# Two more pairs of w_down by seven products: pair 7 also in the first runs of the first two thirds

## The chip, the cores and the metric

The kernel runs on one core of a Trainium2 chip. The metric is the device time of one execution in microseconds, the median of several runs. Five engines matter: TensorE (PE, and PEld for its weight loads), VectorE (DVE), ScalarE (ACT), GpSimd (POOL) and SyncE (SP), whose queue issues nearly all of the DMA transfers.

## The reference

One decoder layer on 256 tokens of width 2048, in float32. An RMS norm feeds one input projection; from its columns come eight attention heads and a pooling mixer; both go through w_out into the residual stream x. Then the part that the change is about:

```python
def conv_ffn(h, w_up, conv_w, conv_b, w_down):
    u = h @ w_up
    ...
    for i in range(CONV_WIDTH):
        y = y + conv_w[i] * u_pad[:, i:i + S]
    gate, val = jnp.split(y, 2, axis=-1)
    return (jax.nn.silu(gate) * val) @ w_down
```

w_up is 2048 x 11264 and w_down 5632 x 2048. The layer's result is x + conv_ffn(rms_norm(x)).

## The kernel before

**Products in three parts.** Every float32 operand is split into a high part, rounded to the format fp32r that TensorE reads fast, and a low part, the rest. A product is then three matmuls: high x high, high x low, low x high. The high part of a weight chunk is written by ScalarE (`high`, L181), the low part by VectorE (`low`, L186), which also releases the chunk's raw tile, so that the next load can start.

**Chunks and steps.** The weights arrive in chunks of 128 x 2048 numbers (1 MB), in an order that `plan` (L71) writes out. There are four raw tiles, and a fifth once the first part of the program has closed. Split chunks lie in four tiles (high) and three tiles (low). The main loop (L1046) goes through steps u, two to a chunk. At a step that begins a chunk it writes, in this order: what is due in `firsts`; `high` of the chunk three ahead and `low` of the chunk two ahead; a `make`, if one is placed there; what is due in `agenda`, where `later(n, f)` puts f for n steps on; what is `deferred`; and then the step's own matmuls. Each engine works in the order written.

**The feed-forward part** goes through the 22 groups of 256 hidden columns in three thirds of 8, 8 and 6 groups (THIRDS). A third first computes its groups (`gate` and `value`, L822 and L836): up-projection, convolution of width 3 over the tokens, SiLU, product, split into high and low parts in the tile hid, where group j is pair j of row blocks of w_down. Then come two runs over the pairs, nb = 0 and nb = 1, one for each half of the 2048 output columns.

**Eight or seven products.** A pair of row blocks and 1024 output columns make a 2 x 2 block product. A dense pair (`eight_products`) issues eight products of 128 x 128 by 128 x 512, 24 matmuls. A pair of the other kind (`seven_mixed` and `seven_rest`) forms seven products in the manner of Strassen and Winograd, 21 matmuls. For that it needs two things:

- Sums of the left factors, four of them, 128 x 128 each (`left_sums`, L874): four operations of VectorE on the tile y of the group, a copy to the high part on ScalarE, and the low part on VectorE.
- Sums of the right factors. `make` (L194) loads a 1 MB block of mix, adds quarters in three operations of VectorE, and stores the result in mixed[i]. It is done ahead, at chunks named in EARLY (before the first third) and PLACES (within the thirds). Later a pair loads it as its "sum" chunk, and then a "rest" chunk of 128 x 1536, one step each. A dense pair loads one chunk of two steps.

SEVEN names the pairs with seven products in each run: pairs 1 to 6 in the first and 1 to 7 in the second run of the first two thirds, 0 to 4 and 0 to 3 in the last third, 35 in all. `down_order` (L66) gives the order: the first run goes through the pairs from 0 up, so that a dense pair 0 comes first and a dense pair 7 last; the second run takes the pairs with seven products first.

**The last group of a third** (pair 7) is finished while the first run is under way. In the last third, where the flag at_once holds, its steps are: the convolution in two halves at steps 2 and 4 of the run, the taps at 6, the product with the gate at 7, the low part of hid at 8. In the first two thirds it goes another way (convolution at once, taps at step 4, product at 6, low part at 8), and the sums of pair 7 follow 16 steps after that, in the second run. The line for it, in `rest2` (L868):

```python
                f = lambda: late.__setitem__(("S", j), left_sums(y, end, at_once))
                later(16, f) if end else f()
```

The sums of all pairs live in six tiles with the tag "sums"; those of pair 7 take the tile that pair 1 has left.

Of the kernel before, what the change touches and what calls it, by code (L numbers as in the profile page):

```python
# [23 lines left out]
F32 = mybir.dt.float32  # L24
# [29 lines left out]
THIRDS = ((0, 8), (8, 16), (16, 22))  # L54
SEVEN = 2 * (((1, 2, 3, 4, 5, 6), (1, 2, 3, 4, 5, 6, 7)),) + (((0, 1, 2, 3, 4), (0, 1, 2, 3)),)
EARLY = (37, 38, 40, 42, 44)
PLACES = ((2, 2.5, 3, 3.5, 4, 4.5, 5, 6, 6.5), (0, 0.5, 1, 1.5, 2, 2.5, 3, 4, 4.5, 5, 6, 6.5), (0, 0.5, 1, 1.5, 2, 2.5, 3, 3.5, 4))
# [7 lines left out]

def down_order(size, sevens, nb):  # L66

    return [*sevens, *(j for j in range(size) if j not in sevens)] if nb else list(range(size))


def plan():  # L71

    rows = [(k, i) for i, k in enumerate(24 * ["tok"] + 25 * ["feat"])]
    makes, t = list(EARLY), 0
    for (g0, g1), sevens, places in zip(THIRDS, SEVEN, PLACES):
        c = rows[-1][1] + 1
        makes += [len(rows) + 4 * int(p) + (5 if p % 1 else 2) for p in places]
        rows += [("feat", c + i) for i in range(4 * (g1 - g0))]
        c = rows[-1][1] + 1
        for nb in range(2):  # L80
            for i, j in enumerate(down_order(g1 - g0, sevens[nb], nb)):
                seven = j in sevens[nb]
                if seven:
                    rows.append(("sum", t))
                    t += 1
                rows.append(("rest" if seven else "tok", c + nb * (g1 - g0) + i))
    assert len(makes) == t, (len(makes), t)
    return rows, makes
# [12 lines left out]
def layer(ctx: ExitStack, tc: tile.TileContext, xT, wts, mix, par, rel_d, ident_d, icnt_d, out):  # L101
# [590 lines left out]
    def open_late():  # L692
        ectx.close()
        pool = ctx.enter_context(tc.tile_pool(name="late", bufs=1))
        late["pool"] = pool
        late["prow"] = pool.tile([P, 8], F32, name="prow", tag="prow")
        late["qrow"] = pool.tile([32, 3, 8], F32, name="qrow", tag="qrow")
        late["x2f"] = [block("x2f").rearrange("p (k t) -> p k t", t=S) for _ in range(4)]
        for k0, k1 in ((0, 2), (2, 4), (4, 8), (8, 12), (12, KT)):
            nc.sync.dma_start(x2_tiles(k0, k1), xT[:, KT + k0 * S:KT + k1 * S].rearrange("p (k t) -> p k t", t=S))  # L700
        late["sq"] = pool.tile([P, 2, S], F32, name="sq2", tag="y1")
        late["u"] = pool.tile([P, 2, 2 + S], F32, name="u")
        nc.gpsimd.memset(late["u"][:, :, :2], 0.0)
        free.append(f"raw{RAWS}")
        load_next()

    def x2_tiles(k0, k1):
# [114 lines left out]
    def gate(ps, g):  # L822
        if g == 0:
            stats2()
        conv_in(ps)

# [9 lines left out]
    def value(ps, g, j, seven, end, at_once):  # L836
# [31 lines left out]
        def rest2(y, hid, ks):  # L868
            nc.vector.tensor_tensor(hid[:, ks, 1, :], y, hid[:, ks, 0, :].bitcast(F32), op=OP.subtract)
            if seven:  # L870
                f = lambda: late.__setitem__(("S", j), left_sums(y, end, at_once))
                later(16, f) if end else f()

    def left_sums(y, alone, at_once):  # L874

        s = y.rearrange("p a (b n) -> p (a b) n", n=P)
        parts = block("sums", F32R).rearrange("p (a b n) -> p a b n", a=2, n=P)
        for out_, a, b, op in ((3, 3, 1, OP.subtract), (1, 0, 1, OP.subtract), (0, 3, 0, OP.add), (2, 2, 0, OP.subtract)):
            nc.vector.tensor_tensor(s[:, out_, :], s[:, a, :], s[:, b, :], op=op)
        pending.append(lambda: nc.scalar.activation(parts[:, 0], s, AF.Copy))  # L880
        low_part = lambda: nc.vector.tensor_tensor(parts[:, 1], s, parts[:, 0].bitcast(F32), op=OP.subtract)
        if alone:
# [4 lines left out]
        else:  # L887
            firsts.setdefault(now[0] + 4, []).append(low_part)
        return parts

# [9 lines left out]
    def seven_mixed(u, j, run, first):  # L900
# [3 lines left out]
        del wparts[c]  # L904
        s2, s3, _, s1 = (tuple(late["S", j][:, a, i, :] for a in range(2)) for i in range(4))
        a22 = tuple(late["hid"][:, 2 * j + 1, a, P:] for a in range(2))
# [6 lines left out]
    def seven_rest(u, j, run, first, last):  # L913
# [4 lines left out]
        a11, a12 = (tuple(late["hid"][:, 2 * j + k, a, :P] for a in range(2)) for k in range(2))  # L918
        s4 = tuple(late["S", j][:, a, 2, :] for a in range(2))
        c0 = run["c"][0]  # L920
# [9 lines left out]
    def seven_sums(run, a):  # L930
# [7 lines left out]
        if run["n"]:  # L938
            b = scratch("sb")
        else:  # L940
            b = late["pool"].tile([P, 2, S], F32, name="sb", tag="y0")
        b = b.rearrange("p a n -> p (a n)")
# [35 lines left out]
    for n, ((g0, g1), sevens) in enumerate(zip(THIRDS, SEVEN)):  # L978
        ups = []
        for g in range(g0, g1):  # L980
            ups.append(feat_block(lambda: late["h"], XK, lambda ps, g=g: gate(ps, g)))
            ups.append(feat_block(lambda: late["h"], XK,
                                  lambda ps, g=g, j=g - g0, sevens=sevens, end=g == g1 - 1: value(ps, g, j, any(j in s for s in sevens), end, sevens[0][0] == 0 and g >= g1 - 2)))
        u0 = len(steps)
# [4 lines left out]
        for nb in range(2):  # L989
# [19 lines left out]
            fresh0 = {(t, b) for t in range(NT) for b in range(2)}  # L1009
            js = down_order(g1 - g0, sevens[nb], nb)  # L1010
            for j in js:
# [68 lines left out]
def chunks(w_in, pool_w, w_out, w_up, w_down):  # L1080
# [27 lines left out]
    for (g0, g1), sevens in zip(THIRDS, SEVEN):  # L1108
        for g in range(g0, g1):
            out += feat(w_up, 256 * g, XK) + feat(w_up, DFF + 256 * g, XK)  # L1110
        for nb in range(2):
            for j in down_order(g1 - g0, sevens[nb], nb):
                out += pair(w_down, 2 * (g0 + j), 1024 * nb, j in sevens[nb])
# [38 lines left out]
```

## Time and profile before

| what | value |
|---|---|
| median of three runs | 984.37 us (984.16 to 985.06) |
| the profiled execution | 984.03 us |
| span of its instructions | 982.2 us |
| PE / DVE / ACT / POOL busy | 977.5 / 873.6 / 628.1 / 60.8 us |
| bytes moved by DMA | 311.31 MB, 317 GB/s on average |
| first, second, last down stage | 78.22, 78.23 and 57.95 us of matmuls, from 458.46, 710.80 and 919.63 us on |

The page gives the busy time of each engine, then 40 slices of the span, the DMA queues, the chain of work that ended last, and the costliest groups of instructions. In a group's line stand the line of the kernel, engine, operation, what it writes and reads, the count, the busy time and the mean length, and the idle time of the engine before it with what ended it. A timeline gives start, length and operation of one engine in order of time; "x2" merges neighbours of one kind, and square brackets show an idle time before the operation.

### The profile page before, as it was taken

The numbers are of one execution on the slowest core, as the hardware profiler recorded it, in microseconds if no ns is written. First come the engines' busy times: TensorE is split into PE (matmuls) and PEld (weight loads), VectorE is DVE, ScalarE is ACT, GpSimd is POOL, SyncE is SP. The second block draws the span as 40 slices with busy tenths as digits, with TensorE's granted clock in tenths as the row PEclk, the third lists the DMA queues.
The fourth block names the chain that finished last, engine by engine and source line by source line (L and its number), as shares of the span: only waits on it lengthen the run. The fifth ranks groups of instructions, "written<-read, shape, count | busy, mean of one in ns | idle before, by whom it ended". The sixth has DMA issues, their size and how long they took to land.

```text
span 982.2 us, 13594 instructions
## 1 busy us (share of the span) xinstructions
PE 977.5 (100%) x5255; PEld 846.4 (86%) x5255; DVE 873.6 (89%) x950; ACT 628.1 (64%) x734; POOL 60.8 (6%) x118
## 2 busy tenths in 40 slices
PE   9999999999999999999999999999999999999998
PEld 7888888898888888888888888888888888888887
DVE  6776859887978999998999999999889999999898
ACT  6655445454556766777766666767686756767762
POOL 0202322200002310000000000000000000000000
PEclk9999999999999999999999999999999999999999
DMA  9959776589968999987999999888779999998684
GB/s 350 317 203 314 244 250 204 204 316 381 333 258 289 303 390 398 361 326 249 353 345 363 343 382 380 355 329 349 268 276 358 371 348 357 386 356 346 211 347 166
DMA packets 51713, 311.31 MB, mean 317 GB/s; under 512 B 7016, under 2 KB 9704, under 8 KB 19904
## 3 DMA queue, kind: packets, MB, share of 16 engines
q1 hardware_dynamic: 46960, 298.51, 80.7%
q0 software_dynamic: 4688, 11.94, 4.1%
q8 instruction: 41, 0.67, 0.3%
q14 instruction: 24, 0.20, 0.1%
HBM read 265.46 MB, written 44.96 MB: 316 GB/s over the span
## 4 chain that ended last, share of the span: by engine, by line
PE 99%; DMA 0%; DVE 0%; SPq 0%; ACT 0%; issue 0%; DVEq 0%
PE ps_feat L271 41%; PE ps_down L894 22%; PE ps_feat L273 21%; PE ps_tok L259 9%; PE ps_val L249 4%; PE ps_pool L280 1%; PE ps_s L492 1%; DMA raw<-in_wts 0%; PE ps_av L528 0%; PE ps_av L530 0%; PE ps_val L240 0%; DVE x L1000 0%; SPq L153 0%; ACT wh L161 0%; PE ps_feat L268 0%; PE ps_row L404 0%
## 5 line engine op out<-in xcount | busy, mean ns | idle before, releaser
L271 PE MATMUL ps_feat<-x2h,wh 128*128 128x512 f32 x1406 | 478.2, 389 | 0.0
L190 DVE TENSOR_TENSOR wl<-raw,wh 128x2048 fp32r<-128x2048 f32 (+1 forms) x180 | 390.4, 2181 | 12.9 <-ACT wh L184 5.2
L184 ACT ACTIVATE wh<-raw 128x2048 fp32r<-128x2048 f32 (+1 forms) x180 | 329.3, 1834 | 99.6 <-DMA raw<-in_wts 52.8
L273 PE MATMUL ps_feat<-x2h,wl 128*128 128x256 f32 x1408 | 389.1, 276 | 0.0
L271 PEld LDWEIGHTS ps_feat<-x2h,wh 128*128 128x128 f32 x1406 | 264.0, 188 | 54.7
L273 PEld LDWEIGHTS ps_feat<-x2h,wl 128*128 128x128 f32 x1408 | 264.3, 188 | 0.0
L894 PE MATMUL ps_down<-wh,hid 128*128 128x512 f32 (+1 forms) x358 | 122.0, 387 | 0.0
L162 DVE TENSOR_TENSOR wl<-raw,wh 128x2048 fp32r<-128x2048 f32 (+3 forms) x44 | 83.0, 1895 | 37.8 <-ACT wh L161 28.9
L894 PE MATMUL ps_down<-wh,sums 128*128 128x512 f32 x280 | 98.6, 389 | 0.0
L540 ACT ACTIVATE fs<-ps_feat 128x512 f32<-128x512 f32 x52 | 31.1, 597 | 105.5 <-PE ps_feat L273 54.4
L271 PE MATMUL ps_feat<-cat,wh 128*128 128x512 f32 x256 | 87.3, 390 | 0.0
L811 ACT ACTIVATE z<-u,pv 128x256 f32<-128x256 f32 x176 | 79.3, 498 | 3.3 <-DVE x L937 3.3
L259 PE MATMUL ps_tok<-wh,xh 128*128 128x512 f32 x256 | 80.1, 392 | 0.0
L894 PEld LDWEIGHTS ps_down<-wh,hid 128*128 128x128 f32 x358 | 67.0, 188 | 13.8
L161 ACT ACTIVATE wh<-raw 128x2048 fp32r<-128x2048 f32 (+3 forms) x44 | 69.3, 1597 | 10.6 <-DMA raw<-in_wts 7.0
L273 PE MATMUL ps_feat<-cat,wl 128*128 128x256 f32 x256 | 70.8, 276 | 0.0
L894 PE MATMUL ps_down<-wl,hid 128*128 128x512 f32 (+1 forms) x179 | 69.3, 387 | 0.0
L819 DVE TENSOR_TENSOR y<-y,z 128x512 f32<-128x512 f32 x88 | 60.6, 688 | 4.4
L894 PEld LDWEIGHTS ps_down<-wh,sums 128*128 128x128 f32 x280 | 52.6, 188 | 10.9
L271 PEld LDWEIGHTS ps_feat<-cat,wh 128*128 128x128 f32 x256 | 48.1, 188 | 9.9
L259 PEld LDWEIGHTS ps_tok<-wh,xh 128*128 128x128 f32 x256 | 48.1, 188 | 9.9
L543 DVE TENSOR_TENSOR fs<-ps_feat,fs 128x512 f32<-128x512 f32 x52 | 35.8, 689 | 22.0 <-ACT fs L540 21.9
(184 smaller groups left out, 1076.2 us busy)
## 6 DMA issues: line engine op xcount, KB each, us to landing
raw<-in_wts SPq DMA_DIRECT2D x143, 1024.0 KB, 7.5
raw<-in_mix SPq DMA_DIRECT2D x35, 1024.0 KB, 7.4
mixed<-raw SPq DMA_DIRECT2D x35, 1024.0 KB, 7.5
raw<-mixed SPq DMA_DIRECT2D x35, 1024.0 KB, 6.2
raw<-in_wts SPq DMA_DIRECT2D x35, 768.0 KB, 6.1
raw<-in_wts SPq DMA_DIRECT2D x4, 512.0 KB, 7.2
x2d<-x2x POOLq DMA_DIRECT2D x4, 512.0 KB, 7.9
x<-x2d POOLq DMA_DIRECT2D x32, 64.0 KB, 6.5
```

Source lines behind the costliest of these rows:

```text
L161: nc.scalar.activation(wh, w, AF.Copy)
L162: nc.vector.tensor_tensor(wl, w, wh.bitcast(F32), op=OP.subtract)
L184: nc.scalar.activation(w, raws[c][:, :width(c)], AF.Copy)
L190: nc.vector.tensor_tensor(wl, raws[c][:, :width(c)], wh.bitcast(F32), op=OP.subtract)
L249: nc.tensor.matmul(ps[b][:, t, :], xh[:, k, a, ts], w[:, ws], start=False, stop=(k == KT - 1 and n == 2), skip_group_check=True)
L259: nc.tensor.matmul(ps[:, t, :], act[:, k0 + k, a, ts], w[:, ws], start=(first and k == 0 and n == 0), stop=(last and k == 1 and n == 2))
L271: nc.tensor.matmul(ps, wh[:, ws], act[:, k, :, :], start=(bool(first) and n == 0), stop=False, skip_group_check=True)
L273: nc.tensor.matmul(ps[:, S:], wl[:, ws], act[:, k, 0, :], start=False, stop=(last and n == len(ks) - 1), skip_group_check=True)
L543: nc.vector.tensor_tensor(dst, ps[:, :, :S], dst, op=OP.add)
L811: nc.scalar.activation(z[i][:, m, :], u[:, m, 1 - i:1 - i + S], AF.Copy, scale=cw[1 - i])
L819: nc.vector.tensor_tensor(y, y, t, op=OP.add)
L894: nc.tensor.matmul(ps, a, w, start=(first and n == 0), stop=(last and n == 2), skip_group_check=True)
```

## The change

Pair 7 becomes a pair with seven products in the first runs of the first two thirds too: 37 sets in all. Both runs of these thirds go through pairs 1 to 7 and then the dense pair 0, so the first run begins with a pair of seven products. Two more makes are needed and are placed at chunks 16 and 27. In the first two thirds the end of a third takes the steps of the last third (at_once holds there too), and the sums of pair 7 follow one step after the low part of hid instead of 16. They lie in two tiles of their own, with the tags "u" (the high part) and "y0" (the low part); so u is made anew in each third, and a scratch tile of the first run takes the tag "y1" instead of "y0".

```diff
-SEVEN = 2 * (((1, 2, 3, 4, 5, 6), (1, 2, 3, 4, 5, 6, 7)),) + (((0, 1, 2, 3, 4), (0, 1, 2, 3)),)
-EARLY = (37, 38, 40, 42, 44)
+SEVEN = 2 * (2 * ((1, 2, 3, 4, 5, 6, 7),),) + (((0, 1, 2, 3, 4), (0, 1, 2, 3)),)
+EARLY = (16, 27, 37, 38, 40, 42, 44)
...
-def down_order(size, sevens, nb):
+def down_order(size, sevens):

-    return [*sevens, *(j for j in range(size) if j not in sevens)] if nb else list(range(size))
+    return [*sevens, *(j for j in range(size) if j not in sevens)]
...
+    def new_u():
+        late["u"] = late["pool"].tile([P, 2, 2 + S], F32, name="u", tag="u")
+        nc.gpsimd.memset(late["u"][:, :, :2], 0.0)
...
     def gate(ps, g):
         if g == 0:
             stats2()
+        elif any(g == g0 for g0, _ in THIRDS):
+            new_u()
...
                 f = lambda: late.__setitem__(("S", j), left_sums(y, end, at_once))
-                later(16, f) if end else f()
+                later(1, f) if end else f()
...
     def left_sums(y, alone, at_once):
...
-        parts = block("sums", F32R).rearrange("p (a b n) -> p a b n", a=2, n=P)
+        if alone:
+            pair = [late["pool"].tile([P, n], F32R, name="sums7", tag=tag)[:, :512] for n, tag in ((516, "u"), (512, "y0"))]
+        else:
+            parts = block("sums", F32R)
+            pair = [parts[:, :512], parts[:, 512:]]
+        pair = [t.rearrange("p (b n) -> p b n", n=P) for t in pair]
...
-            b = late["pool"].tile([P, 2, S], F32, name="sb", tag="y0")
+            b = late["pool"].tile([P, 2, S], F32, name="sb", tag="y1")
...
-                                  lambda ps, g=g, j=g - g0, sevens=sevens, end=g == g1 - 1: value(ps, g, j, any(j in s for s in sevens), end, sevens[0][0] == 0 and g >= g1 - 2)))
+                                  lambda ps, g=g, j=g - g0, sevens=sevens, end=g == g1 - 1: value(ps, g, j, any(j in s for s in sevens), end, g >= g1 - 2)))
```

More of the change, by code (lines that the diff above doesn't have):

```diff
@@ L80, in plan @@
         for nb in range(2):
-            for i, j in enumerate(down_order(g1 - g0, sevens[nb], nb)):
+            for i, j in enumerate(down_order(g1 - g0, sevens[nb])):
                 seven = j in sevens[nb]
@@ L701, in open_late @@
         late["sq"] = pool.tile([P, 2, S], F32, name="sq2", tag="y1")
-        late["u"] = pool.tile([P, 2, 2 + S], F32, name="u")
-        nc.gpsimd.memset(late["u"][:, :, :2], 0.0)
+        new_u()
         free.append(f"raw{RAWS}")
         load_next()
+    def new_u():
+        late["u"] = late["pool"].tile([P, 2, 2 + S], F32, name="u", tag="u")
+        nc.gpsimd.memset(late["u"][:, :, :2], 0.0)
     def x2_tiles(k0, k1):
@@ L824, in gate @@
             stats2()
+        elif any(g == g0 for g0, _ in THIRDS):
+            new_u()
         conv_in(ps)
@@ L871, in rest2 @@
                 f = lambda: late.__setitem__(("S", j), left_sums(y, end, at_once))
-                later(16, f) if end else f()
+                later(1, f) if end else f()
     def left_sums(y, alone, at_once):
         s = y.rearrange("p a (b n) -> p (a b) n", n=P)
-        parts = block("sums", F32R).rearrange("p (a b n) -> p a b n", a=2, n=P)
+        if alone:
[4 more added lines that the diff above has]
+        pair = [t.rearrange("p (b n) -> p b n", n=P) for t in pair]
         for out_, a, b, op in ((3, 3, 1, OP.subtract), (1, 0, 1, OP.subtract), (0, 3, 0, OP.add), (2, 2, 0, OP.subtract)):
             nc.vector.tensor_tensor(s[:, out_, :], s[:, a, :], s[:, b, :], op=op)
-        pending.append(lambda: nc.scalar.activation(parts[:, 0], s, AF.Copy))
-        low_part = lambda: nc.vector.tensor_tensor(parts[:, 1], s, parts[:, 0].bitcast(F32), op=OP.subtract)
+        pending.append(lambda: nc.scalar.activation(pair[0], s, AF.Copy))
+        low_part = lambda: nc.vector.tensor_tensor(pair[1], s, pair[0].bitcast(F32), op=OP.subtract)
         if alone:
@@ L888, in left_sums @@
             firsts.setdefault(now[0] + 4, []).append(low_part)
-        return parts
+        return pair
     def product(ps, left, right, first, last):
@@ L904, in seven_mixed @@
         del wparts[c]
-        s2, s3, _, s1 = (tuple(late["S", j][:, a, i, :] for a in range(2)) for i in range(4))
+        s2, s3, _, s1 = (tuple(t[:, i, :] for t in late["S", j]) for i in range(4))
         a22 = tuple(late["hid"][:, 2 * j + 1, a, P:] for a in range(2))
@@ L918, in seven_rest @@
         a11, a12 = (tuple(late["hid"][:, 2 * j + k, a, :P] for a in range(2)) for k in range(2))
-        s4 = tuple(late["S", j][:, a, 2, :] for a in range(2))
+        s4 = tuple(t[:, 2, :] for t in late["S", j])
         c0 = run["c"][0]
@@ L1009, in layer @@
             fresh0 = {(t, b) for t in range(NT) for b in range(2)}
-            js = down_order(g1 - g0, sevens[nb], nb)
+            js = down_order(g1 - g0, sevens[nb])
             for j in js:
@@ L1111, in chunks @@
         for nb in range(2):
-            for j in down_order(g1 - g0, sevens[nb], nb):
+            for j in down_order(g1 - g0, sevens[nb]):
                 out += pair(w_down, 2 * (g0 + j), 1024 * nb, j in sevens[nb])
```

## The prediction, before the changed kernel ran

> **What bounds the kernel now.** I read the page first, for the busy time of each engine and the chain that ended last.
>
> ```profile
> span 982.2 us, 13594 instructions
> ...
> PE 977.5 (100%) x5255; PEld 846.4 (86%) x5255; DVE 873.6 (89%) x950; ACT 628.1 (64%) x734; POOL 60.8 (6%) x118
> ...
> PE 99%; DMA 0%; DVE 0%; SPq 0%; ACT 0%; issue 0%; DVEq 0%
> ```
>
> TensorE runs from end to end and is 99% of the chain. The list of waits, for TensorE alone, has two lines, both from the start of the program:
>
> ```profile
> PE ps_start L323 <- DVE ones L311: 1.1, 1, 1.1
> PE ps_val L240 <- ACT wh L161: 0.3, 1, 0.3
> ```
>
> So time falls only if TensorE gets fewer matmuls, and rises only if something makes TensorE wait. VectorE, at 89%, is the engine with the least to spare. The chain in order of time gives the three down stages (start, us):
>
> ```profile
> 458.46 78.22 PE ps_down L894 x345
> 710.80 78.23 PE ps_down L894 x345
> 919.63 57.95 PE ps_down L894 x255
> ```
>
> 78.22 / 345 = 0.227 us from one matmul to the next. This is the price I use; the mean of 389 ns that the groups give for such a matmul is its length, and lengths overlap.
>
> **What is removed.** A dense pair issues 24 matmuls of 512 columns, a seven-product pair 21. Pair 7 changes from 24 to 21 in the first run of the first two thirds: 2 x 3 x 0.227 = 1.36 us less on TensorE, all of it on the path. In the Trainium skill, TensorE: Matmul & The Clock Gate, section Back-to-back issue gap, gives about 131 ns as the sustained spacing at 512 columns. By that the saving would be 0.79 us; the rows of this trace have 0.227, and they decide.
>
> **What moves: the sums of pair 7.** These are the left factors of its products, made by VectorE (four small operations, a ScalarE copy to the high part, one operation for the low part). Before, they were made 16 steps later, in the second run, and used there:
>
> ```profile
> 519.43 1.26 DVE L879 TENSOR_TENSOR y<-y 128x128 f32<-128x128 f32 x4
> ...
> 525.41 0.69 DVE L881 TENSOR_TENSOR sums<-y,sums 128x512 fp32r<-128x512 f32 x1
> ```
>
> Now the first run needs them. I count its steps from 0: pairs 1 to 7 take two steps each (0 to 13), pair 0 follows at 14 and 15. Pair 7's up-projection ends just before step 0; by the code its chain goes: convolution from step 2, taps at 6, the product with the gate at 7, low part of hid at 8, the four sums at 9, their low part at 11. At each step VectorE first splits the weight chunk two steps ahead. TensorE wants the low part of the sums as weights of the third matmul of step 12. VectorE works in the order written, so that low part stands behind the splits of chunks 12 and 13. The question is when VectorE gets there.
>
> The first run of the last third is the model: it starts with a seven-product pair already, and its end group runs the same steps up to the low part of hid, without the sums. Its VectorE timeline (start, us, operation, idle before):
>
> ```profile
> 913.67 1.27 DVE L879 TENSOR_TENSOR y<-y 128x128 f32<-128x128 f32 x4
> 914.86 1.75 DVE L190 TENSOR_TENSOR wl<-raw,wh 128x1536 fp32r<-128x1536 f32 x1
> ...
> 920.30 0.69 DVE L543 TENSOR_TENSOR fs<-ps_feat,fs 128x512 f32<-128x512 f32 x1 [2.29 <-ACT fs L540]
> ...
> 921.63 3.95 DVE L190 TENSOR_TENSOR wl<-raw,wh 128x2048 fp32r<-128x2048 f32 x2
> 925.50 0.69 DVE L881 TENSOR_TENSOR sums<-y,sums 128x512 fp32r<-128x512 f32 x1
> 926.10 7.83 DVE L190 TENSOR_TENSOR wl<-raw,wh 128x2048 fp32r<-128x2048 f32 x4
> 934.63 2.29 DVE L190 TENSOR_TENSOR wl<-raw,wh 128x2048 fp32r<-128x2048 f32 x1 [0.70 <-ACT wh L184]
> 936.84 1.41 DVE L819 TENSOR_TENSOR y<-y,z 128x512 f32<-128x512 f32 x2
> 938.17 1.75 DVE L190 TENSOR_TENSOR wl<-raw,wh 128x1536 fp32r<-128x1536 f32 x1
> 939.84 0.68 DVE L843 TENSOR_TENSOR y<-y 128x512 f32<-128x512 f32 x1
> 940.45 2.28 DVE L190 TENSOR_TENSOR wl<-raw,wh 128x2048 fp32r<-128x2048 f32 x1
> 942.65 0.68 DVE L869 TENSOR_TENSOR hid<-y,hid 128x512 fp32r<-128x512 f32 x1
> 943.25 2.28 DVE L190 TENSOR_TENSOR wl<-raw,wh 128x2048 fp32r<-128x2048 f32 x1
> ```
>
> And TensorE there: the run's first matmul, the first one five pairs later, and one place in the second run:
>
> ```profile
> 919.46 0.40 PE L894 MATMUL ps_down<-wh,sums 128*128 128x512 f32 x1
> ...
> 943.29 0.39 PE L894 MATMUL ps_down<-wh,hid 128*128 128x512 f32 x1
> ...
> 953.72 0.48 PE L894 MATMUL ps_down<-wl,sums 128*128 128x512 f32 x1
> 954.03 0.39 PE L894 MATMUL ps_down<-wh,sums 128*128 128x512 f32 x1
> ```
>
> VectorE's side, from start to start in these rows: a split of 2048 takes 2.20 (940.45 to 942.65), of 1536 1.67 (938.17 to 939.84), the four sums 1.19 (913.67 to 914.86). From 943.25 on, the changed kernel does the split of chunk 11 (now 1536 wide, 1.67), the sums (1.19), chunk 12 (2.20), chunk 13 (1.67), the low part (0.69): 7.42, so it ends at 950.67 on the model's clock. TensorE's side: five pairs took 943.29 - 919.46 = 23.83, or 4.77 a pair, so step 12 begins at 919.46 + 28.60 and its third matmul at 948.51. How fast TensorE follows VectorE, and what its weight load adds:
>
> ```profile
> 951.36 2.28 DVE L190 TENSOR_TENSOR wl<-raw,wh 128x2048 fp32r<-128x2048 f32 x1
> ...
> L894 PEld LDWEIGHTS ps_down<-wl,sums 128*128 128x128 f32 x140 | 26.3, 188 | 5.6 <-DVE wl L190 0.2
> ```
>
> That split ended at 953.64, its matmul began at 953.72: 0.08. With 0.19 for the load, the third matmul starts at 950.67 + 0.27 = 950.94 instead of 948.51. **A stall of 2.43 us, in each of two thirds: 4.86 us.** Every later matmul is queued behind it.
>
> Bounds. VectorE stood idle for 0.70 ahead of 934.63, waiting for ScalarE's high part; without that the stall is 1.73. If a weight chunk landed that much later again, 3.1. I take the model's own value, since the order of work is the same.
>
> **What else moves, at nothing.** The two runs start with a seven-product pair instead of a dense one. The model starts so, and its chain of 57.95 us runs through that start unbroken; if that cover were thin, the cost is of the size of the gap after 953.72, under 0.1. The new places of the sums (the buffers of u and of the gate's y, both read out by step 7) and the fresh u of each third are tile names with one memset of two columns on GpSimd, 6% busy. The dense pair at a run's end stands where one stood before.
>
> **What is added: two more makes**, at chunks 16 and 27. Each is one load and one store of 1 MB and three operations of VectorE:
>
> ```profile
> L198 DVE TENSOR_TENSOR raw<-raw 128x1024 f32<-128x1024 f32 x35 | 42.6, 1218 | 0.0
> L200 DVE TENSOR_TENSOR raw<-raw 128x512 f32<-128x512 f32 x35 | 24.2, 692 | 1.2
> L199 DVE TENSOR_TENSOR raw<-raw 128x512 f32<-128x512 f32 x35 | 24.2, 692 | 1.2
> ```
>
> 2.60 us each. Where they fall, and one run to come back to (window, PE, PEld, DVE busy; last DMA share and GB/s):
>
> ```profile
> 88.29:97.79 9.50, 9.50 (x46) 8.00 (x45) 2.29 (x1) 3.86 (x3) 0.00 (x0) 1.00 0.87 322
> 153.00:194.00 41.00, 41.00 (x243) 36.39 (x243) 36.92 (x57) 20.50 (x27) 10.41 (x19) 1.00 0.64 218
> 497.76:531.08 33.32, 33.32 (x149) 27.59 (x147) 32.19 (x26) 23.98 (x15) 0.00 (x0) 1.00 0.95 351
> ```
>
> VectorE is idle for 7.2 of the 9.5 us that follow the first place, and for 4.1 of the 41 after the second; DMA has room in both. SP's queue gets the store, which waits for VectorE there with the next loads behind it, and the raw tile is out of the rotation until it has landed. I cost both at nothing; uncovered it is 2.6 each.
>
> **Sum.** 984.03 (span 982.2 and 1.8 around it) - 1.36 + 4.86 = 987.53 for the profiled execution. The median of the three runs is 0.34 higher: 984.37 + 3.50 = **987.9 us**.
>
> **The rivals.**
>
> No stall (0.13): the low part is there in time, because VectorE's order is not what I read from the code or the wait falls elsewhere. Then only the 1.36 is left: 983.0. Against it: from 934.63 on, VectorE has 16.04 us of work ahead of that tile's end, TensorE gives it 948.51 - 0.27 - 934.63 = 13.61. It decides if 2.4 us of that work stands behind instead of before. This is the way to "not slower". A stall in one third only (0.05) gives 985.4.
>
> Weights land late (0.08). A seven-product pair reads these two:
>
> ```profile
> raw<-mixed SPq DMA_DIRECT2D x35, 1024.0 KB, 6.2
> raw<-in_wts SPq DMA_DIRECT2D x35, 768.0 KB, 6.1
> ```
>
> 1.835 MB in 4.77 us is 385 GB/s for seven pairs in a row, now in both runs, with one dense pair between. The second run before, with the same seven pairs, moved 351 GB/s at a share of 0.95 and TensorE never waited, thanks to what was loaded ahead. Without that stock, 7 x 1.835 MB at 351 takes 36.6 us against 33.3: up to 3.3 more per third, 988 to 994.5, about 991. For it: the share of 0.95. Against: the stall itself gives the loads 2.4 us. The Trainium skill, DMA: Bandwidth & Descriptors, section Where 436 GB/s comes from, sets about 358 GB/s for HBM per core; by that rule seven pairs take 35.9 us and this rival is real. The trace's 351 over a whole run agrees with it.
>
> The makes are not covered (0.04): 2.6 for one, 990.5.
>
> **How the numbers follow.** My forecast has 0.70, with 1.73 to 3.1 a third: 986.5 to 989.2. The range reaches down to the stall in one third, 985.4, and up into the two dearer cases, 990.0; it leaves out no stall (0.13) and about 0.06 above. About 0.2% (1.97 us) is what a measurement of this kernel can tell from no change; slower by more begins at 986.34. The forecast puts 0.67 there and 0.03 below (its low end is only 0.13 above that line), the dearer cases 0.12: slower 0.79. Same: 0.03 + 0.05 + 0.11 of no stall = 0.19. Faster by over 1.97 would need more than the 1.36 that is removed: 0.02.
>
> **What would show it.** Right: the two first down stages 342 matmuls each, some 80.0 us instead of 78.2; a gap of 2.4 us in TensorE's timeline after the second matmul of pair 7 in each first run, ended by L881's operation on VectorE, which comes right behind the split of chunk 13; ends of all other stages as before. Wrong: the low part of pair 7's sums ends before TensorE reaches step 12; a wait of TensorE on weights (L190) in the second runs; any wait of TensorE before 250 us.

## The result, and the profile after

| kernel | median, 12 runs | profiled execution | span |
|---|---|---|---|
| before | 984.41 us | 984.03 us | 982.2 us |
| changed | 993.46 us | 990.43 us | 988.6 us |

The ratio is 1.0082, with a 95% interval of 1.0057 to 1.0107: the change costs 5.6 to 10.5 us. That is slower, as forecast, but by 9.05 us at the medians where 3.5 was worked out, and above the range. Profile and median stand 3 us apart here. The profiled execution was the fastest of the twelve and the only one with a mean TensorE clock of 1.000; the other eleven show 0.996 to 0.999. Against the forecast of 987.53 us for the profiled execution, 990.43 is 2.9 too much.

First the page of the changed kernel: span, busy times, shares of the chain.

```profile
span 988.6 us, 13621 instructions
...
PE 978.5 (99%) x5249; PEld 844.6 (85%) x5249; DVE 882.1 (89%) x958; ACT 630.1 (64%) x736; POOL 61.3 (6%) x120
...
PE 96%; DVE 2%; issue 1%; DMA 0%; ACT 0%; SPq 0%; DVEq 0%
```

TensorE has six matmuls less, as the change says, and the span is 6.4 us longer. VectorE has entered the chain. The list of waits, for TensorE alone, had only the start of the program before; now it begins with two others (us in total, times, longest):

```profile
PE ps_down L904 <- DVE sums L891: 3.5, 2, 1.8
PE ps_down L904 <- DVE wl L190: 1.2, 2, 0.6
```

The chain in order of time shows where. Each of the first two down stages was 78.2 us in one piece before. Now the chain leaves TensorE after 83 matmuls, goes on through work of ScalarE and VectorE that TensorE will wait for, and comes back to TensorE 214 matmuls before the end of the stage; the third stage is whole:

```profile
458.66 19.24 PE ps_down L904 x83
...
486.27 3.96 DVE wl L190 x2
490.22 0.61 DVE sums L891
490.88 48.94 PE ps_down L904 x214
539.82 0.24 PE ps_feat L268 x2
...
713.94 19.19 PE ps_down L904 x83
...
746.15 48.91 PE ps_down L904 x214
...
925.67 58.16 PE ps_down L904 x255
```

539.82 - 458.66 = 81.16 us for the first stage (81.13 for the second), 3.6 more than the 77.55 that 342 matmuls take at 78.22 / 345 each. TensorE's timeline at the break:

```profile
487.39 0.61 PE L904 MATMUL ps_down<-wh,sums 128*128 128x512 f32 x2
488.61 0.50 PE L904 MATMUL ps_down<-wl,sums 128*128 128x512 f32 x1 [0.60 <-DVE wl L190]
490.88 0.74 PE L904 MATMUL ps_down<-wh,sums 128*128 128x512 f32 x2 [1.77 <-DVE sums L891]
491.45 0.39 PE L904 MATMUL ps_down<-wl,sums 128*128 128x512 f32 x1
```

From 487.39 to 491.45 are five spacings, 4.06 us instead of 5 x 0.227 = 1.13: 2.93 us are lost, 0.77 before the second matmul of pair 7 (for the low part of its weight chunk) and 2.04 before the third (for the low part of the sums). Of the other 0.7 of the 3.6, most (0.56) is lost in gaps of up to 0.11 between the run's first matmul at 458.50 and pair 7's first at 487.62, 126 matmuls later. VectorE's timeline of the same run (start, us, operation, idle before):

```profile
460.66 0.69 DVE L891 TENSOR_TENSOR sums<-y,sums 128x512 fp32r<-128x512 f32 x1
461.26 3.95 DVE L190 TENSOR_TENSOR wl<-raw,wh 128x2048 fp32r<-128x2048 f32 x2
466.13 6.16 DVE L190 TENSOR_TENSOR wl<-raw,wh 128x2048 fp32r<-128x2048 f32 x3 [0.92 <-ACT wh L184]
472.21 1.41 DVE L822 TENSOR_TENSOR y<-y,z 128x512 f32<-128x512 f32 x2
473.54 3.96 DVE L190 TENSOR_TENSOR wl<-raw,wh 128x1536 fp32r<-128x1536 f32 x2
477.42 0.68 DVE L848 TENSOR_TENSOR y<-y 128x512 f32<-128x512 f32 x1
478.02 1.75 DVE L190 TENSOR_TENSOR wl<-raw,wh 128x1536 fp32r<-128x1536 f32 x1
480.60 2.29 DVE L190 TENSOR_TENSOR wl<-raw,wh 128x2048 fp32r<-128x2048 f32 x1 [0.83 <-ACT wh L184]
...
490.14 0.69 DVE L891 TENSOR_TENSOR sums<-y,sums 128x512 fp32r<-128x512 f32 x1
```

This is not the order of the last third, on which the prediction was modelled: the low part of pair 6's sums (460.66) comes ahead of the first two splits, the taps (472.21) after five splits instead of seven, and VectorE waits twice for ScalarE. The reason for the order is in one line. The lambda that passes the flag says `g >= g1 - 2`, but only g, j, sevens and end are bound when it is made; g1 is looked up when it runs, after the loop over the thirds has ended, and is 22 then. So at_once holds in the last third alone, before as after, and the edit of this line changes nothing. The section on the change says that at_once holds in the first two thirds too; **that reading was mine and it is wrong.**

### The profile page after: what moved, and what is told of

Same layout as the page of the kernel before. It is cut to its first block, busy times and chain, and to the rows that moved or that the text cites. A ratio compares the mean times of both kernels' runs of the same rounds, so it can differ in the third digit from the quotient of the medians.

```text
span 988.6 us, 13621 instructions
## 1 busy us (share of the span) xinstructions
PE 978.5 (99%) x5249; PEld 844.6 (85%) x5249; DVE 882.1 (89%) x958; ACT 630.1 (64%) x736; POOL 61.3 (6%) x120
## 4 chain that ended last, share of the span: by engine, by line
PE 96%; DVE 2%; issue 1%; DMA 0%; ACT 0%; SPq 0%; DVEq 0%
PE ps_feat L271 41%; PE ps_feat L273 21%; PE ps_down L904 20%; PE ps_tok L259 9%; PE ps_val L249 4%; DVE wl L190 1%; PE ps_pool L280 1%; PE ps_s L492 1%; DMA raw<-in_wts 0%; ACT wh L184 0%; PE ps_av L528 0%; DVE y L889 0%; PE ps_av L530 0%; PE ps_val L240 0%; DVE x L1010 0%
## 5 line engine op out<-in xcount | busy, mean ns | idle before, releaser
L904 PE MATMUL ps_down<-wh,hid 128*128 128x512 f32 (+1 forms) x338 | 116.1, 387 | 0.0
L904 PE MATMUL ps_down<-wh,sums 128*128 128x512 f32 x296 | 104.5, 390 | 3.5 <-DVE sums L891 3.5
L904 PEld LDWEIGHTS ps_down<-wh,hid 128*128 128x128 f32 x338 | 63.3, 188 | 13.2
L904 PEld LDWEIGHTS ps_down<-wh,sums 128*128 128x128 f32 x296 | 55.4, 188 | 15.5 <-DVE sums L891 4.2
L904 PE MATMUL ps_down<-wl,hid 128*128 128x512 f32 (+1 forms) x169 | 65.4, 387 | 0.0
L904 PE MATMUL ps_down<-wl,sums 128*128 128x512 f32 x148 | 58.7, 397 | 1.2 <-DVE wl L190 1.2
```

The source lines that it names most:

```text
L904: nc.tensor.matmul(ps, a, w, start=(first and n == 0), stop=(last and n == 2), skip_group_check=True)
```

## The experiments

Two theories were set against each other first: (A) the stall is VectorE's order of work, made worse by the flag; (B) the time goes to the transfers or the start of the runs. The lowered clock and the makes came up on the way. Edits are against the changed kernel unless a line says otherwise. The kernel before ran beside every group of experiments, at 984.54, 984.67, 984.29 and 984.70 us.

**The flag bound.** It now is what the prediction took it for.

```diff
-  lambda ps, ..., end=g == g1 - 1: value(..., end, g >= g1 - 2)
+  lambda ps, ..., end=g == g1 - 1, late_two=g >= g1 - 2: value(..., end, late_two)
```

> The changed kernel, but the flag at_once is fixed when each group is written, so that the last two groups of the first two thirds really take the plan of the last third (in the changed kernel the flag looks g1 up late and is true in the last third alone). Theory A (VectorE's order makes the stall; the flag made it longer than predicted): TensorE waits 2.2 to 2.4 us at pair 7 in each of the two thirds instead of 3.6, the first two down stages take 79.8 to 80.0 us instead of 81.15, and an execution at full clock takes 987.0 to 987.6 us. Rival B (weights land late because the first run starts with seven-product pairs): the stages stay near 81 us and the time near 990.4. Theory C (what the median of the changed kernel has above its profiled run, 3 us, is TensorE's clock, lowered after the stalls): some runs here show a mean clock below 1 and are 1 to 4 us above the others; without C all runs lie within 1 us.

Measured: 991.09 us, ratio 1.0046 (1.0026 to 1.0065); two runs at 987.07 and 987.17 us with clocks of 1.000 and 0.999, near the 987.53 that the prediction has for the profiled execution, the others 989.2 to 991.8. The profiled execution is the one of 991.77 us, with a mean clock of 0.996. VectorE and TensorE there:

```profile
464.51 0.68 DVE L891 TENSOR_TENSOR sums<-y,sums 128x512 fp32r<-128x512 f32 x1
...
473.88 2.29 DVE L190 TENSOR_TENSOR wl<-raw,wh 128x2048 fp32r<-128x2048 f32 x1 [0.94 <-ACT wh L184]
...
489.22 0.68 DVE L891 TENSOR_TENSOR sums<-y,sums 128x512 fp32r<-128x512 f32 x1
```

```profile
458.47 0.40 PE L904 MATMUL ps_down<-wh,sums 128*128 128x512 f32 x1
...
486.83 0.61 PE L904 MATMUL ps_down<-wh,sums 128*128 128x512 f32 x2
487.68 0.49 PE L904 MATMUL ps_down<-wl,sums 128*128 128x512 f32 x1 [0.24 <-DVE wl L190]
489.95 0.72 PE L904 MATMUL ps_down<-wh,sums 128*128 128x512 f32 x2 [1.77 <-DVE sums L891]
490.52 0.39 PE L904 MATMUL ps_down<-wl,sums 128*128 128x512 f32 x1
```

The low part of the sums ends at 489.90, 31.43 us after the run's first matmul at 458.47. The model had 950.67 - 919.46 = 31.21; the 0.22 more is about what VectorE waits longer for ScalarE here (0.94 against the model's 0.70). From 486.83 to 490.52 are 3.69 us, so 2.56 are lost; the same five spacings of the second third lose 2.84, with a wait for ScalarE of 1.26. The prediction had 2.43. The model came close for this kernel, and this was not the changed kernel. With the flag unbound the same operation ends at 490.83, 32.33 after the first matmul: 0.9 later, about the length of the second wait for ScalarE.

**The low part of pair 7's sums one step earlier**, ahead of the split of chunk 13, with the flag bound.

```diff
-            later(2, low_part)
+            later(1, low_part)
```

> As the kernel with the bound flag, and the low part of pair 7's sums one step earlier, ahead of the split of chunk 13 (1.67 us) instead of behind it. Theory A: the stall falls by 1.7 us to 0.5 to 0.7 us in each third, the first two down stages take 78.0 to 78.3 us, the time is 983.8 to 984.4. Rival B: about the time of the kernel with the bound flag. Theory C: with so short a stall the clock stays at 1.000 in all runs and the runs lie within 1 us.

Measured: 984.91 us, ratio 1.0004 (0.9992 to 1.0016); stages of 78.52 and 78.07, waits of 0.2 to 0.4 left, a mean clock of 1.000 in 9 of 12 runs. One split out of the way takes nearly the whole stall.

**The same low part one step later**, flag as in the changed kernel.

```diff
-            later(2, low_part)
+            later(3, low_part)
```

> The changed kernel with the low part of pair 7's sums one step later, behind one more split of 2048 (2.2 us): a longer wait of TensorE on purpose, the rest as it is. Theory A: the first two down stages are 2.2 us longer each at full clock, 83.4 us, and an execution at full clock takes 994.8 us. Theory C: after a wait of 5 us the clock is halved for 3.4 us in each third in every run, which costs 1.7 us each: mean clock 0.996 to 0.997 in nearly all runs and a median of 997.5 to 998.5 us. Without C the median is 994.8 and the scatter as in the kernel before.

Measured: 998.97 us, ratio 1.0143 (1.0128 to 1.0158); in the profiled execution, the slowest of the four with 1002.78 us, stages of 85.99 and 85.90. TensorE at pair 7:

```profile
491.67 0.49 PE L904 MATMUL ps_down<-wl,sums 128*128 128x512 f32 x1 [0.55 <-DVE wl L190]
496.23 1.22 PE L904 MATMUL ps_down<-wh,sums 128*128 128x512 f32 x2 [4.07 <-DVE sums L891]
```

The wait for the sums grew from 1.77 to 4.07, by 2.30, the length of one split (2.20 from start to start). The rest of the step, 2.5 us a third, is the clock: its record shows 0.5 for 6.83 us behind each stall, twice the stretch that I had expected.

**The order alone**: 35 sets as before and no makes more, but the first runs begin with pair 1 and end with the dense pairs 0 and 7, and the sums of pair 7 are made in the first run.

```diff
-SEVEN = 2 * (2 * ((1, 2, 3, 4, 5, 6, 7),),) + ...
-EARLY = (16, 27, 37, 38, 40, 42, 44)
+SEVEN = 2 * (((1, 2, 3, 4, 5, 6), (1, 2, 3, 4, 5, 6, 7)),) + ...
+EARLY = (37, 38, 40, 42, 44)
```

> The changed kernel with the old 35 sets: pair 7 is dense in the first runs again and the two early makes are left out, but the first runs still start with pair 1 and end with the two dense pairs 0 and 7, and the sums of pair 7 are still made in the first run. Theory A: what remains is a short wait at the start of the run (0.2 to 0.5 us a third, as before pair 7 in the changed kernel): 984.3 to 985.2. Rival B: stages of 80 us or more and 987 to 990, since the start with seven-product pairs is still there.

Measured: 987.50 us, ratio 1.0024 (1.0014 to 1.0033), all clocks 0.999 or 1.000; stages of 79.74 and 79.75, 1.5 us each over those before. The waits of TensorE:

```profile
PE ps_down L904 <- DVE wl L190: 1.2, 2, 0.6
```

This was a miss: I had expected next to nothing. No one waits for the sums of pair 7 here, yet the wait for the chunk ahead of them, 0.6 in each third, and the small gaps are the same as in the changed kernel. So of its 3.6 us a third, 1.5 come from what VectorE does ahead of the sums' low part and 2.04 from the wait for the low part itself.

**Pair 7 reads the low part last.** Of its twelve matmuls in step 12 the three with that operand come at the end.

```diff
+        if j == 7:
+            lows = jobs[3:] + jobs[:3]
+            for a, w, js in ((0, 0, jobs), (1, 0, lows[:1]), (0, 1, jobs), (1, 0, lows[1:])):
+                ...
```

> The changed kernel; only the order of the 12 matmuls of pair 7's first step is another: first the four of high by high, then those with the weights' low parts, and the three with the low part of its sums last. Nothing changes on VectorE. Theory A: the low part of the sums is wanted nine matmuls (2.0 us) into the step instead of two (0.45 us) and the low part of chunk 12 four or five in (1.1 us) instead of one, so the wait of 2.8 us falls to about 1.2 and a third loses 1.6 to 1.8 us instead of 3.6: stages of 79.1 to 79.4 us, 986.3 to 987 at full clock. Theory C (clock): with a wait of 1.2 us nearly all runs keep a mean clock of 1.000, and the median lies within 1 us of that. If the wait were not for these two tiles (rival B), the stages would stay at 81.

Measured: 988.77 us, ratio 1.0044 (1.0032 to 1.0056), all clocks 1.0; stages of 79.71 and 80.01. The wait for the sums shrank from 1.77 to 1.0, and no run shows a lowered clock. The profiled execution also waits 1.5 us in the attention, of which more below.

**The three together**: the edits of the flag, of the low part a step earlier and of the low part read last.

> A version that keeps the change: the flag bound, the low part of pair 7's sums one step earlier, and the three matmuls with it last in the step. Theory A: none of the waits at pair 7 is left, the first two down stages take 77.6 to 77.9 us (342 x 0.227 = 77.5), the profiled execution takes 982.7 to 983.3 and the median is 983.0 to 983.7, 1.0 to 1.4 us under the kernel before; clock 1.000. Rival B: at best the time of the kernel with the low part earlier, stages of 78.1 to 78.5.

Measured: 986.89 us, ratio 1.0023 (1.0010 to 1.0036), runs from 983.91 to 990.72. The stages are 77.74 and 78.02: no stall at pair 7 is left. But the first stage began at 462.16 instead of 458.5, for a reason far away, in the attention:

```profile
PE ps_av L528 <- DMA eT<-e3d: 1.9, 1, 1.9
```

```profile
148.20:151.60 3.40, 3.40 (x12) 2.84 (x12) 2.83 (x15) 1.80 (x8) 0.00 (x0) 0.50 0.79 282
```

The second line is a window of time right behind this wait: 3.4 us at a granted clock of 0.50. The load that was late is queued beside the 1 MB load of the make at chunk 27. A wait at the same matmuls stands in the profiles of four other kernels with that make (0.6 to 1.8 us), not in the changed kernel's own two, nor in those of four others with it, and in none without it.

**Another pair is dense**: pair 7 stays dense in both runs, and pair 0 takes its seven products, so that no run needs sums made in its own course. The smaller scratch only makes room for a seventh tile of sums.

```diff
-SEVEN = 2 * (2 * ((1, 2, 3, 4, 5, 6, 7),),) + ...
+SEVEN = 2 * (2 * ((0, 1, 2, 3, 4, 5, 6),),) + ...
-        ... tag="sums", bufs=6)
+        ... tag="sums", bufs=7)
-    ... dynamic_dma_scratch_size=8192)
+    ... dynamic_dma_scratch_size=4096)
```

> 37 sets of seven products as in the changed kernel, but with pairs 0 to 6 in both runs of the first two thirds, so that pair 7 is the dense pair at the end and needs no sums; a seventh tile for sums, for which the scratch of the GpSimd DMA queue is halved. It has the same matmuls, the same two early makes and the same bytes as the changed kernel. Theory A: no wait of TensorE at pair 7, the first two down stages take 77.6 to 78.0 us (342 x 0.227 = 77.5), the profiled execution 982.7 to 983.3, and all runs are at clock 1.000. Rival B: the stages stay at 80 us or more, and the time above 986.

Measured: 985.20 us, ratio 1.0008 (0.9992 to 1.0024); stages of 78.09 and 78.16, start of the first at 460.63, behind waits of 1.6 and 0.6 us in the early part. The stall is gone, half a microsecond a third of VectorE's order is not. With the flag bound as well (the first diff above):

> Dense pair 7 in both runs again, with the flag bound too, so that the end of a third takes the plan of the last third. In the kernel with dense pair 7 and the flag unbound the first two stages were 0.6 us over 342 x 0.227, in short waits at the start of the run and at chunk 10. Theory A: these come from the order at the start (the low part of pair 6's sums ahead of two splits, the whole convolution ahead of ScalarE's next high part) and go: stages of 77.5 to 77.7 us. If they stay at 78.1, they come from starting with a seven-product pair as such. The early part of the program may again be 2 us longer than before, from the smaller scratch of the GpSimd queue.

Measured: 983.18 us against 984.67, ratio 0.9995 (0.998 to 1.001). The chain:

```profile
458.73 77.54 PE ps_down L904 x342
...
710.40 77.54 PE ps_down L904 x342
```

Both stages are whole, and each is 0.68 us shorter than the 78.22 and 78.23 before: the saving of three matmuls a third, three times 0.227.

**The changed kernel once more**, for the clock.

> The changed kernel once more, for its records of the clock. The first profile (990.43 us) was the one execution of twelve whose clock was 1.000 throughout. Theory: where the mean clock is below 1, the record shows 0.5 for 3.41 us right behind a stall of pair 7 (at about 491 and 747 us), or behind a wait at ps_av (about 148), and each such stretch adds about 1.6 us: 991.5 to 994 for one or two. Rival (the lower mean comes from elsewhere, at the end of the program or spread out): no such stretch at these places.

Measured: 993.11 us, mean clock 0.996. The window of time behind the stall, in the first profile of the changed kernel and then in this one (length, PE, PEld, DVE, ACT, POOL busy, granted clock, DMA share, GB/s):

```profile
491.90:495.30 3.40, 3.40 (x16) 2.79 (x15) 3.11 (x2) 2.00 (x3) 0.00 (x0) 1.00 0.96 320
```

```profile
491.90:495.30 3.40, 3.40 (x9) 2.63 (x8) 2.24 (x2) 1.22 (x2) 0.00 (x0) 0.50 0.95 320
```

Nine matmuls instead of sixteen. Its timeline there has one every 0.43 us instead of every 0.23:

```profile
491.98 0.63 PE L904 MATMUL ps_down<-wl,hid 128*128 128x512 f32 x1
492.41 0.63 PE L904 MATMUL ps_down<-wh,hid 128*128 128x512 f32 x1
492.84 0.63 PE L904 MATMUL ps_down<-wh,sums 128*128 128x512 f32 x1
```

The record of the clock gives 0.5 for 3.41 us from 491.9 and again from 747.9 on. The stages are 82.72 and 82.75, so 1.56 and 1.62 more than in the first profile. The twelve runs of the changed kernel fit this roughly: the two with a mean clock of 0.998, about one such stretch, took 991.20 and 991.59 us, the eight with 0.996 or 0.997 took 993.07 and more. Two of the eight, 996.04 and 1001.36 us, are later than two such stretches explain, and why was not found.

**The makes.** The kernel before with two makes more, at chunks 16 and 27, that nothing reads; then with one of them (`makes + [16]`, `makes + [27]`); then with room for two more blocks in memory and no make (the second diff, and two more blocks in the input mix):

```diff
-    return rows, makes
+    return rows, makes + [16, 27]
```

```diff
-    mixed = [dram.tile(...) for i in range(len(makes))]
+    mixed = [dram.tile(...) for i in range(len(makes) + 2)]
```

> The kernel before with two makes more, at chunks 16 and 27, whose results nothing reads; the sets, the order and everything else as before. Theory: the make at chunk 27 puts a load of 1 MB on SP's queue at 132.8 us, beside the loads of the last attention heads' probabilities (eT, GpSimd's queue, 134 to 139 us). In some executions these then land at 146 instead of 141 us and TensorE waits 0.6 to 2 us for them at ps_av (L528), sometimes with the clock halved behind it. So: down starts between 458.3 and 462.2 us, not the same in each profile; median 984.5 to 988, runs spread over 3 us or more, some with a clock below 1. Rival, the prediction's own step (the makes cost nothing): median 984.2 to 984.9, runs within 1.5 us of each other as those of the kernel before, no wait at ps_av, start 458.3 to 458.5.

> The kernel before with one make more, at chunk 16 (its result is read by nothing). The two makes together took 985.55 us against 984.29, with runs from 984.28 to 987.36. Theory (the cost is that of the make at chunk 27, whose load lies beside the loads of the probabilities): this one costs nothing, 984.0 to 984.7, runs within 1.5 us. Rival (each make costs the same, by one more tile taken from the loads): 984.9, half of the 1.26, with a spread of 1.5 to 3 us.

> The kernel before with one make more, at chunk 27. Theory (this make is the one that costs): 985.2 to 986.5, runs spread over 2 us or more, and where the profiled run is above 985.5, a wait at ps_av (L528) on the load of eT. Rival (each make costs the same): 984.9. Second rival (neither costs alone, the data that both add does): 984.0 to 984.7.

> The kernel before with room for two more blocks in the input mix and in the store mixed, and no make more: no instruction differs, only where the data lies in the chip's memory. Theory (makes cost by their transfers): as the kernel before, 984.0 to 984.7, ratio 1 within 0.001. Rival (what spread the runs is where the data lies): 985 to 986 and runs spread over 2 us or more, as with the two makes.

Measured: both makes 985.55 against 984.29 us, ratio 1.0013 (1.0004 to 1.0022), runs spread over 3.1 us; its profile has no wait at the attention but late loads in a second run (waits of 0.2 and 0.4 for splits near 503 and 528 us). Then 984.92, 985.14 and 985.07 against 984.70; their ratios (0.9987, 0.9987 and 0.9988, each with an interval of about 0.0025 to either side) hold 1. Room alone moved the median as much as either make. So neither my theory that the make at chunk 27 is the one that costs, nor the rival of a fixed price for each, is borne out, and what spread the times of the two together stays open. By its interval the kernel with both takes 0.4 to 2.2 us more; how much of that is the makes' own price is not shown.

Last, the two early makes moved behind the attention, into the up-projection of the first third (chunks 54 and 58), for the kernel with pair 7 dense and for the one with three mends; and, for the former, the one at chunk 27 moved to chunk 33:

```diff
-EARLY = (16, 27, 37, 38, 40, 42, 44)
-PLACES = ((2, 2.5, 3, ...
+EARLY = (37, 38, 40, 42, 44)
+PLACES = ((0.5, 1.5, 2, 2.5, 3, ...
```

```diff
-EARLY = (16, 27, 37, 38, 40, 42, 44)
+EARLY = (16, 33, 37, 38, 40, 42, 44)
```

> The kernel in which pair 7 is dense in both runs and pair 0 takes its seven products, with the two early makes moved from chunks 16 and 27 into the first third, behind the attention (0.5 and 1.5 in its list of places, chunks 54 and 58). Theory (the load at chunk 27 is what scatters its times): no wait at ps_av, start 458.3, stages 77.5, median 982.3 to 983.2 and every run below 984.5, unless the first third has no room for them (VectorE: 2.6 us each; then the stage of its up-projection grows by up to 5). Rival (the scatter is of the chip, not of the makes): some runs again at 985 to 992, with or without the move.

> The changed kernel with the flag bound, the low part of the sums a step earlier, the matmuls that read it last, and the two early makes moved to chunks 54 and 58. Theory: the stall at pair 7 is gone (stages 77.7 to 78.0) and so is the wait at ps_av: start 458.3 to 458.6, median 983.3 to 984.3, runs within 1.5 us. Rival (the start of down at 462.16 in the run without the move has another cause): start again 460 to 462 and median 985.5 to 988.

> The kernel in which pair 7 is dense in both runs, pair 0 takes its seven products and the flag is bound (983.18 us, 9 of 12 runs at 982.6 to 983.5, the others to 991.9), with the make at chunk 27 moved to chunk 33, so that its load comes behind the probabilities of heads 4 and 5 and ahead of those of 6 and 7. Theory (the late runs come from the load at chunk 27): median 982.5 to 983.2 and no run above 984; faster than the kernel before by 0.1 to 0.2%. Rival (they come from elsewhere): the same median with 2 to 4 of 12 runs above 984. If chunk 33 has no room for a make: a wait between 165 and 200 us and 984 to 986.

Measured: 989.99 (ratio 1.0056, 1.0044 to 1.0068) and 990.76 us (1.0076, 1.0053 to 1.0098), both misses: the wait at the attention is gone, but there is no room in the first third. TensorE's waits in the first of the two:

```profile
PE ps_feat L273 <- DVE wl L190: 4.0, 5, 1.7
```

At chunk 33: 983.14 against 984.70, ratio 0.9976 (0.9947 to 1.0005), with 9 of 12 runs at 982.6 to 983.3 and three above 984, one of them at 992.6, as without the move. So the late runs are not those of the load at chunk 27; the kernel before had such runs too in that group (three of 35 above 993).

The kernel with pair 7 dense and the flag bound is the best of this study. Its intervals hold 1, because of these single late runs; but in its two versions 18 of 24 runs lie between 982.5 and 983.6, under the lowest of the 58 runs of the kernel before beside them (983.81).

## Why the prediction was right and wrong

**What is removed: right.** 0.227 a matmul and 1.36 in all; 2 x 0.68 where nothing waits. The skill's spacing of 131 ns (TensorE: Matmul & The Clock Gate, Back-to-back issue gap, in the Trainium skill) would have given 0.39 a third; the trace has 0.68.

**The place of the stall: right.** The third matmul of step 12, the low part of the sums, behind the splits of chunks 12 and 13; the second runs of these thirds never waited, and the chain's last stage is unbroken. Not foreseen was the wait of 0.77 one matmul earlier, for the low part of chunk 12. Moving the low part by one split in either direction moved the stall by one split.

**The size of the stall: wrong, at the step "I take the model's own value, since the order of work is the same."** It was not, because of the flag. With the order that I had assumed, 2.43 was worked out and 2.56 and 2.84 measured; that the first comes so close is in part luck, since the low part came 0.22 later than in the model and TensorE followed it 0.22 sooner. With the real order it is 3.6 a third: 2.9 at pair 7 and 0.7 elsewhere, mostly ahead of it. The upper bound of 3.1 rested on the same model and fell with it. Evidence against it lay in the profile of before: its VectorE timeline in the first third could have been set beside that of the last. There, too, the low part of the sums stands ahead of the splits, and the taps come after four splits:

```profile
460.46 0.69 DVE L881 TENSOR_TENSOR sums<-y,sums 128x512 fp32r<-128x512 f32 x1
461.06 1.75 DVE L190 TENSOR_TENSOR wl<-raw,wh 128x1536 fp32r<-128x1536 f32 x1
...
470.84 1.41 DVE L819 TENSOR_TENSOR y<-y,z 128x512 f32<-128x512 f32 x2
```

And the flag's old form looks up the same variable.

**A term was missing: the clock.** The prediction says that every later matmul is queued behind the stall, and takes for granted that they follow at 0.227. In eleven runs of twelve the mean clock was below 1 (0.999, as one of them has, can come from the program's end alone: with pair 7 dense and the flag bound the record shows 0.5 only from 980.20 on, behind the last matmul), and in the execution of this kind that was profiled eight matmuls behind each stall followed at half speed. With this the sum of that execution closes. The measured terms are differences of the same two stages, so what the closing shows is that next to nothing was lost elsewhere:

| term, us | forecast | measured | from |
|---|---|---|---|
| matmuls removed | -1.36 | -1.36 | pair 7 dense, flag bound |
| stall under the assumed order | +4.86 | +5.4 | flag bound, 2.56 + 2.84 |
| the real order of VectorE | 0 | +1.8 | 81.16 + 81.13 - 2 x 77.55 - 5.4 |
| halved clock behind the stalls | 0 | +3.2 | the changed kernel twice |
| sum | +3.5 | +9.0 | span: 991.3 - 982.2 = 9.1 |

**The start of the runs with a seven-product pair: right at nothing** with the flag bound (pair 7 dense: not one gap in a stage), not with the real order, where the small gaps of up to 0.11 are.

**The 0.27 from VectorE's end to the matmul: wrong, too dear by 0.2.** The low part ends at 490.14 + 0.69 = 490.83 and the matmul begins at 490.88: 0.05 in all, with no 0.19 for the weight load on top.

**The makes at nothing:** not shown wrong in the changed kernel, whose two profiles start the first down stage at 458.66 and 458.47 us, against 458.46 before, and show no wait at the attention (the first waits 0.7 us more than before at ps_val, L240, early in the program, the second not). In other kernels with them there is a wait in the attention in some executions. Open, within the 2.2 us above.

**The rivals.** Weights landing late did not happen: in the stretch that the prediction gives for the second run, more was moved than before (356 against 351 GB/s) at a smaller share, and TensorE did not wait there:

```profile
497.76:531.08 33.32, 33.32 (x149) 27.55 (x148) 31.29 (x23) 20.88 (x13) 0.00 (x0) 1.00 0.93 356
```

Nor was it the stall that gave the loads their time: with pair 7 dense and the flag bound, the 37 sets leave no gap in the first two down stages. No stall, 983.0, is what that kernel gives (983.18). The range left out both things that happened, since every case in it was built on one order of work and on one clock.

## What to carry to other kernels

Before a stage is taken as the model of another, lay the two timelines beside each other, and follow each flag to the value it has when it is read, above all in a closure that runs after its loop. On an engine that works in the order written, a small operation behind two large ones costs their length to whoever waits for it: move it ahead of one, or arrange the work so that no one needs it in time. And a stall of 2 us or more on TensorE is to be priced with a second term, the slow matmuls behind it; in this kernel that was 1.6 us where it came.

## What the runs showed of the hardware

**The clock falls after stalls of about 2 us, not in every execution.** The same kernel with the same gaps (0.77 and 2.04, 0.71 and 2.04) kept its clock in one profile and had it halved in the next, for 3.41 us each time, at a price of 1.6 us. One wait of 1.9 was enough in the attention, while waits of 1.8 (low part one step later) and 1.5 (read last) at the same place were not; two of 4.3 and 0.7 us halved it for 6.83; where no gap in these stages was longer than 1.2 us (the low part earlier, or read last, or not needed), no profile shows a lowered clock there.

**What goes with it is where the stall falls on a grid of 3.41 us.** Within each record the clock changes only at points a whole number of 3.413 us apart: 491.86 and 747.86 in the second profile of the changed kernel are 75 steps apart. The first profile has one change, at 987.66, behind its last matmul; 146 steps before it lies 489.31. Cut at these points, the two windows around the stall in the first profile, and then the window of the stall and the next one in the second profile, read (columns as above):

```profile
485.90:489.31 3.41, 2.61 (x11) 1.59 (x9) 3.38 (x4) 2.93 (x3) 0.00 (x0) 1.00 0.94 321
489.31:492.72 3.41, 1.84 (x8) 1.54 (x9) 3.41 (x3) 2.78 (x2) 0.00 (x0) 1.00 1.00 370
```

```profile
488.45:491.86 3.41, 1.63 (x6) 1.16 (x7) 3.41 (x3) 3.15 (x2) 0.00 (x0) 1.00 1.01 379
491.86:495.27 3.41, 3.41 (x10) 2.64 (x9) 2.25 (x2) 1.23 (x2) 0.00 (x0) 0.50 0.92 314
```

In the first profile the stall is split over two windows, with 0.80 and 1.57 us in which TensorE is idle (the length less PE busy; 1.50 and 0.85 in the second third). In the second profile most of it lies in one window, with 1.78 us (2.38 in the second third), and the next window has half the clock. Over all the profiles of this study, a window at full clock with 1.86 us or more of idle time is followed by half the clock and one with 1.67 or less is not; between these, two were (1.77 and 1.78) and two were not (1.82 and 1.84). The two executions of the changed kernel have their stall at nearly the same time (its end is at 490.88 and 490.68), but lie 0.86 us apart on the grid (489.31 against 488.45). That is how the same stall can cost 1.6 us more in one execution and nothing more in another. It is read from the profiles; no run moves the program against the grid to test it.

The Trainium skill, TensorE: Matmul & The Clock Gate, section What's actually happening, says that the gate watches the engine's activity in windows of 3413 ns that run freely; the stretches of 3.41 us agree, and so does the grid. The same page, section Wait — 56ns, not 53.3ns?, gives 426.7 ns from one matmul to the next at the halved clock; the trace's 0.43 us agrees. Its section HAM oscillation — how this bites in real kernels sums up the rule as no idle gaps over about 3.4 us; by that none of the changed kernel's stalls would have lowered the clock, and here the measurement decides.

**Late transfers come in some executions only.** In one profile the last of the loads of the attention's probabilities landed 5 us later than in another of a kernel with the same makes (at 146.7 instead of 141.5), with the DMA engines busier at that time. It was issued at 138.8 instead of 136.7, so 2.1 of the 5 us were lost before it started:

```profile
132.00:146.00 14.00, 14.00 (x71) 11.86 (x70) 3.64 (x3) 5.10 (x6) 4.38 (x8) 1.00 0.73 258
```

```profile
132.00:146.00 14.00, 12.99 (x62) 10.71 (x61) 3.65 (x3) 4.78 (x5) 4.36 (x8) 1.00 0.93 313
```

The first is the changed kernel, the second the one with three mends, in the same stretch of time: a share of 0.73 against 0.93. What made the difference was not found.
